# Mixer B of a hybrid encoder: a projection piece ahead of each odd step's transposes, q's transposes behind a piece, and the PSUM pools of the dense stages in the other order

## The chip, the cores and the metric

One core of one Trainium2 chip runs the whole program. The metric is the device time of one execution in microseconds (us); less is better. The engines are named PE (TensorE, matmuls; PEld is its weight load), DVE (VectorE), ACT (ScalarE), POOL (GpSimd) and SP (SyncE, which issues most DMAs here). PSUM is the memory that PE writes; it has eight banks of 128 x 512 fp32.

## The reference

Two layers over 1024 tokens of width 1024. Layer 0 uses mixer A (neighbourhood attention over a 16 x 64 grid), layer 1 mixer B (grouped-query attention). After each mixer stands a dense stage.

```python
for i in range(DEPTH):                                   # DEPTH = 2
    h = rms_norm(x, norm_g[i])
    y = mixer_a(h, ...) if i % 2 == 0 else mixer_b(h, ...)
    x = x + y                                            # y = (o * silu(gate)) @ w_out
    g = sigmoid(rms_norm(x, ple_norm_g[i]) @ ple_w_gate[i])
    x = x + g * (p[i] @ ple_w_proj[i])
return rms_norm(x, final_norm_g)

def mixer_b(h, ...):                                     # 16 query heads, 4 k/v heads, head size 64
    q, k, v, gate = split(h @ w_in)                      # 1024, 256, 256, 1024 columns
    q, k = rope(rms_norm(q)), rope(rms_norm(k))
    o = softmax(q @ k.T / 8) @ v                         # all 1024 tokens see all 1024
    return (o * silu(gate)) @ w_out
```

## The kernel before

Products are made in fp32r with each operand split in a high and a low half (names ending in h and l, or KA and KB): a product is high x high, high x low and low x high. ACT makes a high half by a copy, DVE the low half by a subtraction. The weights come by DMA into `wstage`, ACT splits off `wh` (L226) and DVE `wl` (L231).

The stages follow each other: mixer A, `dense_phase(0)`, mixer B, `dense_phase(1)`. Each opens its own PSUM pools, and pools take banks in the order in which they are opened. Mixer A opens `d` (2 banks), `s` (2), `t` (2) and then `o` (2); mixer B `d` (1 bank), `s` (2 tiles of 2 banks), `t` (2 tiles of 1 bank) and `o` (1); a dense stage `t` (4) and `d` (4). The first four blocks of a dense stage (`strassen_out`) are written to `d` tiles, the next four to `t` tiles.

**Mixer B** goes through 128 steps; a step is one query head, one half of the tokens and one block of 128 queries. Step n has these parts:

- scores, `f_S`: four matmuls of 128 x 512 into an `s` tile (KA, then KB), and DVE's minimum over it (`mn`, L1198). They are issued two steps ahead: step n issues those of n+2.
- exponentials, `f_E`: ACT, from `s` to `P` (L1204), issued one step ahead.
- transposes, `f_T`: eight transposes of `P` into two `t` tiles (L1214), each tile copied by ACT to PTh (L1216), and the rest by DVE to PTl (L1217).
- PV, `f_AV`: at every even n, for the steps n-2 and n-1 together, eight matmuls with PTh and eight with PTl into the `o` tile of the head (`o<-PTh,V` and `o<-PTl,V`). A new `o` tile is opened for every head and half, so at every second PV. When the head is done, ACT copies a part of it (L519) and DVE joins it (`Y<-o,Y`, L483), some items later.
- `q_stack`, at every eighth step: four transposes of q into one `t` tile (L1168), ACT's copy of it (L1170), and some items later the scaled halves QS by ACT (L1177) and DVE (L1178).

An even step issues: PV, exponentials of n+1, transposes of n, scores of n+2. An odd step issues: transposes of n, exponentials of n+1, scores of n+2, and at n = 3, 11, 19, ... a q_stack.

Between these, `mix(att, dense)` places **pieces** of other PE work: the projections of the next q, k and v (twelve matmuls of 128 x 256, half of a token tile), of the gates and of p (six matmuls of 128 x 512, L606 is ACT's copy of the last kind). All are written to the one `d` tile; the last piece of a tile is followed by ACT's copies (L1080 and L1044 for q, L1136 for k and v). Items of `att` and pieces have weights (`CB` for even steps with PV, `CN` for others; 1300 to 1316 for a piece), and after each item as many pieces follow as keep the two sums in proportion. The four calls of `mix` take 32 steps each, with 24, 50, 32 and 32 pieces. In the last one the last `HOLD` = 2 pieces are kept for behind the last step. Each item is followed by `pulse()`, which counts down the timers of `post`, the queue of deferred small operations. `leave` defers the copies of a finished piece behind an exponential that comes next.

After the steps `strassen_out` of the dense stage begins with `block(Y[0], ...)`; before mixer B, `dense_phase(0)` ends with transposes of the normalised rows by `to_ht` (L467, ACT's copy L468, DVE's subtraction L469); the last of these transposes are issued between mixer B's first pieces (`kv_items`).

Of the kernel before, what the change touches and what calls it, by code (L numbers as in the profile page):

```python
# [18 lines left out]
PSUM = bass.MemoryType.PSUM  # L19
# [20 lines left out]
HOLD = 2  # L40
# [118 lines left out]
def trunk(ctx, tc, x, wts, rpb, gains, hgains, mask, rope, gain0, out):  # L159
# [183 lines left out]
    def pulse():  # L343
        WQ.pump()
        post.tick()
# [13 lines left out]
            while self.left:  # L359
                self.left.pop(0)()  # L360

    leave = Evac()

    def mix(att, dense, lead=0, hold=0):
        for f, _ in dense[:lead]:
            f()
            pulse()
        kept = dense[len(dense) - hold:]
        dense = list(dense[lead:len(dense) - hold])
        total = sum(c for _, c in dense)  # L370
        span = sum(c for _, c in att)
        spent = done = 0.0
        for i, (f, c) in enumerate(att):
            f()
            leave.run()
            pulse()
            done += c
            while dense and spent < total * done / span - 1e-6:
                leave.run()
                leave.wait = i + 1 < len(att) and getattr(att[i + 1][0], "first", False)  # L380
                d, c = dense.pop(0)
                d()
                leave.wait = False
                spent += c
        leave.run()
        for f, _ in dense + kept:
            f()
            pulse()
# [598 lines left out]
    def mixer_b(pend):  # L987
        with ExitStack() as es:
# [174 lines left out]
            def q_stack(pair, hf):  # L1163
                g = pair // 2
                ps = psT.tile([128, 4, 128], F32, name="t")
                c = slice((pair % 2) * 128, (pair % 2) * 128 + 128)
                for t in range(4):
                    pe.transpose(ps[:, t], QT[g, hf][:, t, c], ident)  # L1168
                raw = sb.tile([128, 512], F32, name="th")
                act.activation(raw, ps.rearrange("p t c -> p (t c)"), AF.Copy)  # L1170
                for j in range(2):
                    own, oth = slice(64 * j, 64 * j + 64), slice(64 - 64 * j, 128 - 64 * j)
                    qs = sb.tile([128, 512], F32R, name="QS", bufs=3)
                    QST[2 * pair + j, hf] = qs

                    def high(qs=qs, own=own, oth=oth):
                        act.activation(qs[own], raw[own], AF.Copy)  # L1177
                        post.add(DQ, lambda: dve.tensor_tensor(qs[oth], raw[own], qs[own], ALU.subtract))  # L1178
                    if pro[0]:
                        high()  # L1180
                    else:
                        post.add(QO[j], high)
# [3 lines left out]
            steps = [(2 * p + j, hf, t) for p in range(8) for hf in range(2) for j in range(2) for t in range(4)]  # L1186

            def f_S(h, hf, t):
                g = h // 4
                ps = psS.tile([128, 1024], F32, name="s")  # L1190
                qt = QST[h, hf][:, t * 128:(t + 1) * 128]
                for kk, kt in enumerate((KA[g], KB[g])):
                    for c in range(2):
                        mm(ps[:, c * 512:(c + 1) * 512], qt, kt[:, c * 512:(c + 1) * 512], kk == 0, kk == 1)
                if t == 0:
                    RS[h, hf] = sb.tile([128, 4], F32, name="rs", bufs=3)
                mn = sb.tile([128, 1], F32, name="mn", bufs=3)
                dve.tensor_reduce(mn, ps, axis=AX.X, op=ALU.min)  # L1198
                P[h, hf, t] = (ps, mn)

            def f_E(h, hf, t):
                ps, mn = P[h, hf, t]
                p = sb.tile([128, 1024], F32, name="P")
                act.activation(p, ps, AF.Exp, bias=mn, scale=-1.0, accum_out=RS[h, hf][:, t:t + 1])  # L1204
                P[h, hf, t] = p

            def f_T(h, hf, t):
                p = P.pop((h, hf, t))
                c = slice((t % 2) * 128, (t % 2) * 128 + 128)
                for b in range(2):  # L1210
                    ps = psT.tile([128, 4, 128], F32, name="t")
                    for i in range(4):
                        k = 4 * b + i
                        pe.transpose(ps[:, i], p[:, k * 128:(k + 1) * 128], ident)  # L1214
                    ks = slice(4 * b, 4 * b + 4)
                    act.activation(PTh[:, ks, c], ps, AF.Copy)  # L1216
                    dve.tensor_tensor(PTl[:, ks, c], ps, PTh[:, ks, c], ALU.subtract)  # L1217
# [4 lines left out]
            def f_AV(h, hf, t):  # L1222
                if t == 1:
                    OP[h, hf] = psO.tile([128, 512], F32, name="o")
                o = OP[h, hf][:, (t - 1) * 128:(t + 1) * 128]
                for k in range(NT):
                    mm(o, V[h // 4][:, k], PTh[:, k], t == 1 and k == 0, False)
                for k in range(NT):
                    mm(o, V[h // 4][:, k], PTl[:, k], False, t == 3 and k == NT - 1)
                if t == 3:  # L1230
                    fin = head_end(sb, h, hf, RS[h, hf], OP.pop((h, hf)), ylive, 1, gg, talloc)
                    if fin:
                        later.add(FIN[1], fin)
# [18 lines left out]
            def exps(n):  # L1252
                def f():
                    f_E(*steps[n])
                f.first = True
                return f
            for g in range(4):
                att = []
                for n in range(32 * g, 32 * g + 32):
                    h, hf, t = steps[n]  # L1260
                    av = n >= 2 and n % 2 == 0
                    w = CB if av else CN
                    def turn():
                        if WQ.gate:
                            WQ.gate = False
                        later.tick()
                    att.append((turn, w[0]))
                    if av:
                        att.append((lambda n=n: f_AV(*steps[n - 1]), w[1]))
                    te = [(lambda n=n: f_T(*steps[n]), w[2])]  # L1270
                    if n + 1 < len(steps):
                        te.append((exps(n + 1), w[3]))
                    if n % 2 == 0 and n > 0:
                        te.reverse()
                    att += te
                    if n + 2 < len(steps):
                        def scores(n=n):
                            f_S(*steps[n + 2])
                            WQ.gate = n % 2 == 1 if n < 112 else None
                        att.append((scores, w[4]))  # L1280
                    m = n + QS_AT
                    if m % 8 == 0 and m < len(steps):
                        hn, fn, _ = steps[m]
                        att.append((lambda hn=hn, fn=fn: q_stack(hn // 2, fn), 0.0))
                    if YLOAD_B <= n < YLOAD_B + NT:
                        att.append((lambda t=n - YLOAD_B: load_y(1, t), 0.0))
                if g == 3:
                    att.append((lambda: f_AV(*steps[-1]), CB[1]))
                def gates(p):
                    return [i for hf in range(2) for i in gate_items("bg", p, hf, dalloc, sb, gg)]  # L1290
                dense = []
                if g > 0:
                    dense += left
                if g < 3:
                    qi = q_items(g + 1, pool)
                    kv = kv_items(1, pool) if g == 1 else [None, None]
                    dense += kv[:-2] + qi[:KS] + [k for k in kv[-2:-1] if k] + qi[KS:8] + [k for k in kv[-1:] if k] + gates(2 * g + 1) + qi[8:]
                    left = gates(2 * g + 2)
                else:
                    WQ.cap[3] = 2  # L1300
                    dense += gates(2 * g + 1) + pp_items(1, dalloc, sb, TAGS_B)
                mix(att, dense, hold=HOLD if g == 3 else 0)
            post.flush()
            later.flush()
            post.flush()
# [182 lines left out]
    def dense_phase(l):  # L1488
        with ExitStack() as es:
            one = es.enter_context(tc.tile_pool(name="done", bufs=1))  # L1490
            ps_t = es.enter_context(tc.tile_pool(name="dpt", bufs=4, space=PSUM))
            ps_d = es.enter_context(tc.tile_pool(name="dps", bufs=4, space=PSUM))
            wp2 = es.enter_context(tc.tile_pool(name=f"wp2{l}", bufs=2))
            X = [one.tile([128, D], F32, name=f"X{t}") for t in range(NT)]
            WQ.alloc[2] = lambda: [wp2.tile([128, 1024], F32R, name=f"w{c}2") for c in "hl"]
# [263 lines left out]
```

## Time and profile before

| | us |
|---|---|
| median of 3 timed runs | 1531.45 |
| lowest and highest of them | 1528.62, 1531.79 |
| the profiled execution, its own time | 1530.75 |
| its span, first to last instruction | 1528.9 |
| PE busy in it | 1499.4 (98%) |
| VectorE busy in it | 1102.1 (72%) |
| ScalarE busy in it | 899.4 (59%) |

In a row of the timeline stand the start and the duration in us, engine, line and operation, what is written and read, and how many instructions are merged into the row; in brackets the idle time of the engine just before, and what ended it. Matmuls overlap each other, so the duration of a row is longer than the time by which it puts off the next one. A row of waits gives total us, how often, and the longest. A row of stretches gives the bounds, the length, then busy time and instructions of PE, PEld, DVE, ACT and POOL, the granted clock of PE, the DMA engines' busy share and GB/s.

### The profile page before, as it was taken

How to read it: one execution, taken by the hardware profiler on the slowest of the kernel's cores; microseconds unless marked ns; L12 is line 12 of the kernel's file. 1: busy time of each engine (PE TensorE's matmuls, PEld its weight loads, DVE VectorE, ACT ScalarE, POOL GpSimd, SP SyncE). 2: the span in 40 equal slices, each digit the busy share in tenths (PEclk: the TensorE clock that was granted, in tenths of full speed). 3: DMA queues.
4: the chain of work that ended last, by engine and by line, in shares of the span. 5: the costliest groups of instructions: out<-in, count | busy, mean ns of one | idle time of the engine just before them, and what ended most of it. 6: DMA issues, size and time to landing. Idle time of an engine off the chain costs nothing.

```text
span 1528.9 us, 24361 instructions
## 1 busy us (share of the span) xinstructions
PE 1499.4 (98%) x8976; PEld 1314.0 (86%) x8976; DVE 1102.1 (72%) x2091; ACT 899.4 (59%) x1801; POOL 304.4 (20%) x413
## 2 busy tenths in 40 slices
PE   8999999999999999999999999999999999999997
PEld 8888988988988888888988889989899888878786
DVE  7566576477477599767887786777877877789856
ACT  6565465466366635433467676676767777745432
POOL 1222232142112000010222132453141300000022
PEclk9999999999999999999999999999999999999999
DMA  8325355272122962262210111111101122763123
GB/s 256 119 95 140 83 142 162 63 165 85 36 87 66 334 247 97 90 201 79 77 49 21 32 39 50 46 32 43 58 27 47 37 77 70 234 225 115 67 88 134
DMA packets 91096, 157.22 MB, mean 103 GB/s; under 512 B 18144, under 2 KB 54112, under 8 KB 90464
## 3 DMA queue, kind: packets, MB, share of 16 engines
q1 hardware_dynamic: 85824, 139.66, 27.9%
q0 software_dynamic: 2560, 8.39, 3.2%
q10 hardware_dynamic: 2592, 7.61, 1.4%
q8 instruction: 71, 1.16, 0.3%
q14 instruction: 49, 0.40, 0.1%
HBM read 125.10 MB, written 50.83 MB: 115 GB/s over the span
## 4 chain that ended last, share of the span: by engine, by line
PE 80%; DVE 11%; ACT 5%; issue 2%; DMA 1%; SPq 0%; ACTq 0%; DVEq 0%
PE d L317 50%; PE o L317 10%; PE s L317 8%; PE t L1214 6%; PE t L758 3%; DVE PTl L1217 2%; PE t L317 1%; PE t L467 1%; DVE mn L1198 1%; DVE xn L1541 1%; ACT PTh L1216 1%; ACT P L1204 1%; ACT wh L226 1%; DVE X L1437 1%; DVE HTl L1383 1%
## 5 line engine op out<-in xcount | busy, mean ns | idle before, releaser
L317 PE MATMUL d<-wh,HTh 128*128 128x256 f32 (+1 forms) x1032 | 343.3, 335 | 6.0 <-DVE HTl L469 2.3
L317 PE MATMUL d<-wh,HTl 128*128 128x256 f32 (+1 forms) x1032 | 338.3, 330 | 0.3 <-DVE HTl L469 0.3
L317 PE MATMUL d<-wl,HTh 128*128 128x256 f32 (+1 forms) x1032 | 337.0, 328 | 0.0
L1217 DVE TENSOR_TENSOR PTl<-t,PTh 128x512 fp32r<-128x512 f32 x256 | 164.4, 683 | 111.4 <-ACT PTh L1216 111.1
L317 PEld LDWEIGHTS d<-wh,HTh 128*128 128x128 f32 x1032 | 195.1, 190 | 25.8 <-DVE HTl L469 2.5
L317 PEld LDWEIGHTS d<-wl,HTh 128*128 128x128 f32 x1032 | 194.9, 190 | 19.0
L317 PEld LDWEIGHTS d<-wh,HTl 128*128 128x128 f32 x1032 | 195.1, 190 | 18.7 <-DVE HTl L469 0.5
L317 PE MATMUL d<-HTh,wh 128*128 128x512 f32 x504 | 206.0, 409 | 0.0
L317 PE MATMUL d<-HTh,wl 128*128 128x512 f32 x504 | 198.3, 394 | 0.0
L317 PE MATMUL d<-HTl,wh 128*128 128x512 f32 x504 | 197.6, 392 | 0.0
L1204 ACT ACTIVATE P<-s,mn 128x1024 f32<-128x1024 f32 x128 | 142.8, 1116 | 67.5 <-DVE mn L1198 66.7
L1216 ACT ACTIVATE PTh<-t 128x512 fp32r<-128x512 f32 x256 | 139.7, 593 | 45.1 <-PE t L1214 44.6
L1198 DVE TENSOR_REDUCE mn<-s 128x1 f32<-128x1024 f32 x128 | 154.7, 1209 | 12.3 <-PE s L317 12.3
L1214 PE MATMUL t<-ident,P 128*128 128x128 f32 x1024 | 137.2, 275 | 4.8 <-DVE PTl L1217 1.7
L317 PE MATMUL s<-KA,QS 128*128 128x512 f32 (+2 forms) x384 | 133.7, 402 | 0.0
L1214 PEld LDWEIGHTS t<-ident,P 128*128 128x128 f32 x1024 | 114.7, 140 | 20.1 <-DVE PTl L1217 12.6
L231 DVE TENSOR_TENSOR wl<-wstage,wh 128x1024 fp32r<-128x1024 f32 x78 | 101.7, 1308 | 34.7 <-ACT wh L226 34.2
L317 PE MATMUL s<-KB,QS 128*128 128x512 f32 (+2 forms) x384 | 121.8, 371 | 0.0
L317 PE MATMUL o<-PTh,V 128*128 128x256 f32 (+2 forms) x672 | 118.9, 288 | 1.2 <-DVE Y L483 0.9
L317 PE MATMUL o<-PTl,V 128*128 128x256 f32 (+2 forms) x672 | 119.1, 288 | 0.1
L762 DVE TENSOR_TENSOR PTl<-t,PTh 128x384 fp32r<-128x384 f32 (+1 forms) x128 | 66.6, 520 | 71.3 <-ACT PTh L761 70.1
L317 PEld LDWEIGHTS d<-HTh,wl 128*128 128x128 f32 x504 | 94.7, 188 | 21.6
(237 smaller groups left out, 2700.9 us busy)
## 6 DMA issues: line engine op xcount, KB each, us to landing
wstage<-in_wts SPq DMA_DIRECT2D x88, 512.0 KB
pp<-ppD SPq DMA_DIRECT2D x32, 256.0 KB
X<-in_x SPq DMA_DIRECT2D x15, 512.0 KB
rb<-rD SPq DMA_DIRECT2D x56, 128.0 KB
ppD<-th SPq DMA_DIRECT2D x20, 256.0 KB
tD0t<-in_wts SPq DMA_DIRECT2D x16, 256.0 KB
tD1t<-in_wts SPq DMA_DIRECT2D x16, 256.0 KB
xD<-X SPq DMA_DIRECT2D x8, 512.0 KB
```

Of the source, the lines that this page charges most:

```text
L226: act.activation(hi, s, AF.Copy)
L231: eng.tensor_tensor(lo[:, c:c + n], s[:, c:c + n], hi[:, c:c + n], ALU.subtract)
L317: pe.matmul(ps, a, b, start=first, stop=last, skip_group_check=True)
L467: pe.transpose(ps[:, k], xn[:, (4 * c + k) * 128:(4 * c + k + 1) * 128], ident)
L758: pe.transpose(ps[:, i], sp[:, i * 128:(i + 1) * 128], ident)
L762: dve.tensor_tensor(PTl[:, sl], ps[:, :m], PTh[:, sl], ALU.subtract)
L1198: dve.tensor_reduce(mn, ps, axis=AX.X, op=ALU.min)
L1204: act.activation(p, ps, AF.Exp, bias=mn, scale=-1.0, accum_out=RS[h, hf][:, t:t + 1])
L1214: pe.transpose(ps[:, i], p[:, k * 128:(k + 1) * 128], ident)
L1216: act.activation(PTh[:, ks, c], ps, AF.Copy)
L1217: dve.tensor_tensor(PTl[:, ks, c], ps, PTh[:, ks, c], ALU.subtract)
L1383: dve.tensor_tensor(al(t + m, c), src[m], ah(t + m, c), ALU.subtract)
```

## The change

`blocks(n)` names a step's transposes: "blocks" for even n, "apart" for odd n. `mix` notes in `since` whether a piece has come since the last transposes. Ahead of an "apart" item with none since, it issues the next piece; when no other piece is left, one of the kept ones, as long as more than two are there. That piece counts as spent. `HOLD` of the last call is raised by one. `after` is a second deferring queue that always waits: a q_stack goes into it and is issued behind the next piece, or at the end of the call. In `dense_phase`, the `d` pool is opened ahead of the `t` pool.

```diff
-    leave = Evac()
+    leave, after = Evac(), Evac()
+    after.wait = True
 
     def mix(att, dense, lead=0, hold=0):
         ...
+        since = True
         for i, (f, c) in enumerate(att):
+            kind = getattr(f, "kind", None)
+            if kind == "apart" and not since and (dense or len(kept) > 2):
+                d, e = (dense or kept).pop(0)
+                d()
+                spent += e
+                after.run()
+            if kind in ("apart", "blocks"):
+                since = False
             f()
             leave.run()
             pulse()
             done += c
             while dense and spent < total * done / span - 1e-6:
                 ...
                 d()
                 leave.wait = False
                 spent += c
+                since = True
+                after.run()
         leave.run()
+        after.run()
         for f, _ in dense + kept:
             f()
             pulse()
         ...
+            def blocks(n):
+                def f():
+                    f_T(*steps[n])
+                f.kind = "apart" if n % 2 else "blocks"
+                return f
         ...
-                    te = [(lambda n=n: f_T(*steps[n]), w[2])]
+                    te = [(blocks(n), w[2])]
         ...
-                        att.append((lambda hn=hn, fn=fn: q_stack(hn // 2, fn), 0.0))
+                        att.append((lambda hn=hn, fn=fn: after(lambda: q_stack(hn // 2, fn)), 0.0))
         ...
-                mix(att, dense, hold=HOLD if g == 3 else 0)
+                mix(att, dense, hold=HOLD + 1 if g == 3 else 0)
         ...
     def dense_phase(l):
+            ps_d = es.enter_context(tc.tile_pool(name="dps", bufs=4, space=PSUM))
             ps_t = es.enter_context(tc.tile_pool(name="dpt", bufs=4, space=PSUM))
-            ps_d = es.enter_context(tc.tile_pool(name="dps", bufs=4, space=PSUM))
```

## The prediction

> **What bounds the kernel now.** I read the page's busy shares first, then the busy time of the stretch that the change reorders (mixer B's 128 steps, 777 to 1344 us), then who waits for whom, then PE's timeline there and at the three hand-overs between stages.
>
> ```profile
> PE 1499.4 (98%) x8976; PEld 1314.0 (86%) x8976; DVE 1102.1 (72%) x2091; ACT 899.4 (59%) x1801; POOL 304.4 (20%) x413
> 777.00:1344.00 567.00, 557.83 (x3808) 501.51 (x3807) 423.58 (x663) 402.21 (x747) 137.90 (x212) 1.00 0.18 57
> PEld t L1214 <- DVE PTl L1217: 12.6, 36, 1.3
> ```
>
> TensorE bounds nearly everything: 98% busy, in mixer B 557.83 of 567 us, at full clock (1.00). VectorE has 423.58 us of work there and ScalarE 402.21, so neither is full, but each is the second link of a short loop. A step's eight transposes (L1214) fill the two PSUM tiles `t`; ScalarE copies each to PTh (L1216), VectorE subtracts to PTl (L1217), and only then is a `t` tile free. The third row is what that costs where it shows: the load of the next transposes waited 36 times, 12.6 us in all. There is no other large pot, so what can be won is waits of tenths of a microsecond, many times over.
>
> Busy time hides such waits, because matmuls overlap; I therefore count from start to start. A step that does not wait (T 20, scores, a piece, T 21, scores), and then one wait:
>
> ```profile
> 860.65 0.71 PE L317 MATMUL s<-KA,QS 128*128 128x512 f32 x2
> 861.66 0.28 PE L317 MATMUL d<-wh,HTh 128*128 128x256 f32 x1
> 863.09 1.04 PE L1214 MATMUL t<-ident,P 128*128 128x128 f32 x8
> 863.88 0.71 PE L317 MATMUL s<-KA,QS 128*128 128x512 f32 x2
> 865.59 1.19 PE L317 MATMUL o<-PTh,V 128*128 128x256 f32 x8 [0.54 <-DVE Y L483]
> ...
> 864.76 0.68 DVE L483 SCALAR_TENSOR_TENSOR Y<-o,Y 64x512 f32<-64x512 f32 x1
> ```
>
> Scores take 1.01 (861.66 - 860.65), a piece 1.43, transposes 0.79. The scores at 863.88 take 1.71, so PV waited 0.70: it opens a new `o` tile, of which there is one, and VectorE's join of the old head (L483) ended at 865.44.
>
> **The change part by part.** *Pieces ahead of an odd step's transposes.* Nothing is added or removed on any engine; pieces change places. I worked mix()'s two budgets through with the weights CB, CN and the pieces' costs. Group 0 has 24 pieces on 16 pairs of steps, so every second pair has none between its two transposes; group 1 has 50 and group 2 has 32, and there nearly every pair has one already; group 3 has 32 less those held. So "apart" puts a piece forward in only ten places: n = 1, 5, 9, 13, 17, 101, 113, 115, 125, 127. In the order of before, the transposes of n and n+1 have only the scores between them at n = 0, 4, 8, 12, 16, 102, 104 and 124, and nothing at all at 126; after it, at none of these. n = 8 is the usual one, 124 the worst of the eight:
>
> ```profile
> 810.75 1.04 PE L1214 MATMUL t<-ident,P 128*128 128x128 f32 x8
> 811.54 0.70 PE L317 MATMUL s<-KA,QS 128*128 128x512 f32 x2
> 812.75 1.26 PE L1214 MATMUL t<-ident,P 128*128 128x128 f32 x8
> ...
> 1328.35 0.71 PE L317 MATMUL s<-KA,QS 128*128 128x512 f32 x2
> 1330.19 1.25 PE L1214 MATMUL t<-ident,P 128*128 128x128 f32 x8 [0.67 <-DVE PTl L1217]
> 1332.44 0.67 DVE L483 SCALAR_TENSOR_TENSOR Y<-o,Y 64x512 f32<-64x512 f32 x1
> 1333.61 1.11 PE L317 MATMUL o<-PTh,V 128*128 128x256 f32 x8
> ```
>
> At n = 8 the scores take 1.21 instead of 1.01 (the first tile is late) and the transposes 1.26 instead of 1.04 (the second is): 0.42 lost. A piece of 1.43 covers both. Six places at 0.42 (4, 8, 12, 16, 102, 104): **2.5**. At n = 124 it is 0.83 + 0.21, but PV 125 then meets the join, which ends at 1333.11 against PV's start at 1333.61; that leaves **0.4**. The ends:
>
> ```profile
> 777.85 0.71 PE L317 MATMUL s<-KA,QS 128*128 128x512 f32 x2
> 780.19 0.98 PE L1214 MATMUL t<-ident,P 128*128 128x128 f32 x7 [1.16 <-ACT P L1204]
> 778.93 1.11 ACT L1204 ACTIVATE P<-s,mn 128x1024 f32<-128x1024 f32 x1
> 778.10 1.22 DVE L231 TENSOR_TENSOR wl<-wstage,wh 128x1024 fp32r<-128x1024 f32 x1 [0.26 <-PE t L1214]
> ...
> 1336.90 1.03 PE L1214 MATMUL t<-ident,P 128*128 128x128 f32 x8
> 1339.02 1.25 PE L1214 MATMUL t<-ident,P 128*128 128x128 f32 x8 [1.08 <-DVE PTl L1217]
> 1340.42 1.33 PE L317 MATMUL o<-PTh,V 128*128 128x256 f32 x8
> ```
>
> At n = 0 the wait is for the exponentials of step 1, to 780.04. The piece put ahead needs the low half of its weights, which VectorE has at 779.32, so it starts its second matmul about 0.5 late, and of the 1.33 between 778.86 (777.85 + 1.01, scores done) and 780.19 the net is **0.9** (0.9 to 1.3). At 126 the transposes take 2.12 instead of 0.79; a third held piece goes between: **1.3**. T 127 to PV 127 (1.40) stays: that is the copy's own latency. Together 5.1.
>
> The same order puts PV right behind its step's scores where a piece stood between: ten new places (1, 5, 9, 13, 17, 99, 111, 113, 115, 125). Such a place exists at n = 21 (0.70 lost, above) and at n = 25, where nothing is lost:
>
> ```profile
> 880.45 0.71 PE L317 MATMUL s<-KA,QS 128*128 128x512 f32 x2
> 881.47 0.76 PE L317 MATMUL o<-PTh,V 128*128 128x256 f32 x5
> ```
>
> So 0 to 7.0. The two differ in VectorE's queue: at 21 a query's low half (L1178, 0.69) stands ahead of the join. The change moves that too (next part), and at n = 9 to 17 and 111 to 115 it isn't there; I take **0.8**, for the weight splits in group 3.
>
> *q's transposes behind a piece.* All 15 q_stack calls now run behind the next piece, 2 to 6 turns of the post queue later. Their four transposes use one `t` tile, freed by ScalarE's copy:
>
> ```profile
> 789.40 0.71 PE L317 MATMUL s<-KA,QS 128*128 128x512 f32 x2
> 790.77 0.63 PE L1168 MATMUL t<-ident,qt 128*128 128x128 f32 x4 [0.20 <-DVE PTl L1217]
> 791.16 0.36 PE L317 MATMUL d<-wh,HTh 128*128 128x256 f32 x1
> 791.44 0.60 ACT L1170 ACTIVATE th<-t 128x512 f32<-128x512 f32 x1
> 792.87 0.38 ACT L1080 ACTIVATE qt<-d 128x256 f32<-128x256 f32 x1 [0.83 <-PE d L317]
> 793.28 0.42 ACT L1044 ACTIVATE t<-qt 128x256 f32<-128x256 f32 x1
>   DVE PTl L1217: 3.8, 8
> ```
>
> Removed: the wait ahead of q (1.37 instead of 1.01 here; 3.8 us in eight idles by PE and its weight load together, which partly overlap): **3.3**. Added: in seven places (48, 72, 80, 88, 96, 104, 112 by the head they serve) the piece behind which q now goes stands right ahead of a step's transposes. Those need both tiles, and the second is q's. The copy starts 0.67 after q and takes 0.60, so the tile is free 1.27 after q starts, and is wanted at 0.39 (q) + 0.40 = 0.79: 0.5 lost. Where that piece ends its tile (80, 96), its own evacuation (0.38 + 0.42) goes first on ScalarE, from about 0.2 behind the piece, and the loss is about 0.85; at 48 it is a k/v tile with a third copy, about 1.1. Four at 0.5, two at 0.85, one at 1.1: **4.8**. The deferred scaling to QS (L1177, L1178) still comes eight turns or more before the scores that read it; and coming later it leaves the join's place, so most of the present PV waits (0.70 at n = 21, and its like at 29 and 101) go: **1.2**, between 0 and 1.5. The rope-table loads on SP that a piece issues move with it by one item; POOL, 137.90 busy of 567, waits for them, and PE does not.
>
> *PSUM pools of the dense stages.* Pools take banks in the order they are opened. Before, `t` had banks 0-3 and `d` 4-7; after, the reverse. What matters is whose bank the next stage's first tile falls on.
>
> ```profile
> 708.20 0.60 PE L467 MATMUL t<-ident,xn 128*128 128x128 f32 x4
> 711.11 0.39 PE L317 MATMUL d<-wh,HTh 128*128 128x256 f32 x1 [2.31 <-DVE HTl L469]
> 710.37 0.69 DVE L469 TENSOR_TENSOR HTl<-t,HTh 128x512 fp32r<-128x512 f32 x1
> ...
> 530.14 0.60 ACT L606 ACTIVATE G<-d 128x512 f32<-128x512 f32 x1 [1.27 <-PE d L317]
> 530.72 0.69 DVE L536 TENSOR_TENSOR Y<-Y,t 128x512 f32<-128x512 f32 x1
> 531.51 0.47 PE L317 MATMUL d<-wh,HTh 128*128 128x512 f32 x1 [1.46 <-ACT G L606]
> ...
> 1346.32 0.40 PE L317 MATMUL d<-wh,HTh 128*128 128x512 f32 x1
> 1346.57 0.60 ACT L606 ACTIVATE th<-d 128x512 f32<-128x512 f32 x1 [1.79 <-PE d L317]
> ```
>
> Dense stage 0 to mixer B (708 us): B's first k/v piece is in bank 0, which the last `t` tile of the dense stage holds until VectorE's L469 ends at 711.06. Afterwards bank 0 was a `d` tile released three tiles ago, and the piece can start when the transposes are issued, about 708.65: **2.4** (2.0 if the whole `d` pool has to be free). The next pieces and the transposes shift with PE; ScalarE's and VectorE's work there hangs on PE's. Mixer A to dense stage 0 (531 us): the first block is on bank 4, mixer A's `t`, read by L536 until 531.41; afterwards on bank 0, free with L606 at 530.74: **0.7** (1.45 if it is the other of two `d` tiles). Mixer B to dense stage 1 (1346 us): now bank 4 is free and the block starts at once; afterwards bank 0 is the `d` tile that the last piece fills, free with L606 at 1347.17: **0.9 lost**. The Trainium skill (Perfetto Trace Analysis, section Matmuls) says that independent matmul groups should rotate through different PSUM banks, so that the evacuation of one runs beside the matmuls of the next. It speaks against the new order at the last of these places, where the trace bears it out; read for itself it would count both mixer ends as losses and put this part at 2.4 - 0.7 - 0.9 = 0.8 instead of 2.2.
>
> **Sum.** 5.1 - 0.8 + 1.2 + 3.3 - 4.8 + 2.2 = 6.2 us less. The profiled execution took 1530.75 (span 1528.9), so 1524.5; the three timed runs have a median of 1531.45 and span 1528.62 to 1531.79, so the profiled one stands 0.7 under the median, well inside them. I keep **1524.5**. About 0.2% (3.1 us) is what a measurement can tell from no change.
>
> **The rivals.**
> 1. *The next link takes over.* With TensorE ahead, each of the odd steps meets VectorE's join or ScalarE's copies instead: the 2.5 + 0.4 and the 1.2 are not had. For it: at n = 124 and 21 the join is what ends last. Against it: at n = 8 PV started well behind it. 1530.75 - 6.2 + 4.1 = 1528.7. Chance 0.15.
> 2. *The swap of pools frees nothing.* If B's first piece waits at 708 for something else that ends with L469, the 2.4 and the 0.7 go and the 0.9 is paid: 1530.75 - 6.2 + 3.1 = 1527.7. For it: one row names L469 and none names the bank. Against: the start stands 0.05 behind L469's end, and that instruction's output is not read by this piece. Chance 0.12.
> 3. *Slower: q's copy jams the odd transposes.* In the seven places q's tile is the second one of the transposes right behind it. If ScalarE has an exponential (1.11) and a piece's evacuation ahead of the copy, each costs 0.5 + 1.11 + 0.8 = 2.4, so 16.8 instead of 4.8: 1530.75 - 6.2 + 12.0 = 1536.6. Without q the rest gains 11.0, so it decides from 11.0 / 7 = 1.6 a place; over 0.2% slower from 2.0. Against it: the exponential of that step is issued behind the transposes, and the earlier one ahead of the even step's. Chance 0.10.
> 4. *Moved, not removed.* Each piece put forward is missing a step later, and the ten new PV places each pay the 0.70 of n = 21: 1530.75 - 6.2 + 6.2 = 1530.7, no change. Chance 0.10.
>
> **How the numbers follow.** The forecast has 0.53. Faster by over 0.2% (under 1527.7) holds nearly all of it (0.51), half of rival 2, a third of rival 1 and little of the others: 0.66. Slower holds most of rival 3 and the tails of 1 and 4: 0.11. No change: 0.23. The low end takes the good bounds together: 0.4 more at n = 0, 0.6 at 124, 0.3 at the joins, 0.75 at 531, 0.8 at the new PV places and 1.8 at q (all seven at 0.5, and the whole 3.8 removed): 4.7 lower, 1519.8, rounded down to 1519.5. The high end reaches over rivals 1 and 2 up to rival 4's edge: 1530. Rival 3 and half of rival 4 are left out.
>
> **What would show it.** The first k/v piece at about 0.45 behind the last transposes of dense stage 0 and no wait on L469 there; the first block of dense stage 1 about 0.9 behind the last piece, waiting for ScalarE's L606. In mixer B no L1214 start 1.2 behind scores at n = 4, 8, 12, 16; the pot of waits on L1217 down from 12.6 to about 6; L1168 no longer waiting for L1217, but in seven places transposes waiting for ScalarE's L1170, 0.5 to 1.1 each. Wrong would be: PV waiting for L483 in more places than now, L1170 waits over 1.6 each, or a wait of 2 us left at the start of mixer B.

## The result, and the profile after

| | before | after |
|---|---|---|
| median of six runs, us | 1531.37 (1528.62 to 1531.79) | 1524.69 (1523.32 to 1526.17) |
| ratio to before, 95% interval | | 0.9961 (0.9951 to 0.9971) |
| profiled execution, its span, us | 1530.75, 1528.9 | 1525.28, 1523.4 |

By the ratio the kernel became 6.0 us faster (4.4 to 7.5 by the interval; the two medians are 6.7 apart); the forecast was 6.2 less, or 1524.5. The profile page's row of busy times after, and two rows of who waits for whom:

```profile
PE 1496.9 (98%) x8976; PEld 1314.9 (86%) x8976; DVE 1096.4 (72%) x2091; ACT 899.8 (59%) x1801; POOL 303.8 (20%) x413
...
PEld t L1227 <- DVE PTl L1230: 6.7, 17, 1.3
PEld t L1227 <- ACT th L1183: 4.5, 7, 1.0
```

Lines have moved by 13: the transposes are L1227, PTl L1230, q's transposes L1181, their copy L1183. PE does the same work as before (x8976). The pot of waits on PTl is about halved (12.6 us in 36 waits before), and a new one has come: seven waits on the copy of q. Written T n for the first transposes of step n, mixer B wins 5.6 us from T 0 to T 35, loses 2.8 from there to T 98, and wins 1.0 from there to T 127.

The three hand-overs between stages in PE's timeline, each the start of the old stage's last matmul or transposes and of the new stage's first matmul. After:

```profile
529.49 0.39 PE L317 MATMUL d<-wh,wl 128*128 128x512 f32 x1
530.62 0.50 PE L317 MATMUL d<-wh,HTh 128*128 128x512 f32 x1 [0.74 <-ACT G L619]
...
707.32 0.60 PE L480 MATMUL t<-ident,xn 128*128 128x128 f32 x4
708.17 0.39 PE L317 MATMUL d<-wh,HTh 128*128 128x256 f32 x1 [0.25 <-ACT th L1617]
...
1339.63 0.39 PE L317 MATMUL d<-wh,KB 128*128 128x512 f32 x1
1340.75 0.50 PE L317 MATMUL d<-wh,HTh 128*128 128x512 f32 x1 [0.74 <-ACT th L619]
```

Of before, the two last matmuls whose followers the prediction shows:

```profile
529.67 0.39 PE L317 MATMUL d<-wh,wl 128*128 128x512 f32 x1
...
1346.09 0.39 PE L317 MATMUL d<-wh,KB 128*128 128x512 f32 x1
```

Mixer A to dense stage 0 takes 1.13 instead of 1.84, dense stage 0 to mixer B 0.85 instead of 2.91, mixer B to dense stage 1 1.12 instead of 0.23: 0.71 and 2.06 won, 0.89 lost.

Step 8 after, with a piece between scores and transposes, then PV behind the scores of step 11; and step 126:

```profile
806.01 1.03 PE L1227 MATMUL t<-ident,P 128*128 128x128 f32 x8
806.80 0.70 PE L317 MATMUL s<-KA,QS 128*128 128x512 f32 x2
809.23 1.04 PE L1227 MATMUL t<-ident,P 128*128 128x128 f32 x8
810.02 0.71 PE L317 MATMUL s<-KA,QS 128*128 128x512 f32 x2
811.03 1.11 PE L317 MATMUL o<-PTh,V 128*128 128x256 f32 x8
...
1330.26 1.03 PE L1227 MATMUL t<-ident,P 128*128 128x128 f32 x8
1332.65 1.03 PE L1227 MATMUL t<-ident,P 128*128 128x128 f32 x8
1334.04 1.23 PE L317 MATMUL o<-PTh,V 128*128 128x256 f32 x8 [0.35 <-ACT PTh L1229]
```

From 806.80 to 809.23 are 2.43: scores (1.01) and a piece (1.42), no wait; both sets of transposes take 0.79. PV follows 1.01 behind its scores, and the join (L496, from 809.79 for 0.68) ended at 810.47, ahead of it. At 126 transposes, piece and transposes take 3.78 to PV; less 1.40 for the piece that is 2.38 instead of 3.52, so 1.14 won.

Where q lands right ahead of transposes (T 44, behind a k/v piece):

```profile
961.07 0.60 PE L1181 MATMUL t<-ident,qt 128*128 128x128 f32 x4
961.33 0.38 ACT L1149 ACTIVATE th<-d 128x256 f32<-128x256 f32 x1 [1.13 <-PE d L317]
961.50 0.60 PE L1227 MATMUL t<-ident,P 128*128 128x128 f32 x4
...
962.25 0.57 ACT L1183 ACTIVATE th<-t 128x512 f32<-128x512 f32 x1
962.88 0.66 PE L1227 MATMUL t<-ident,P 128*128 128x128 f32 x4 [0.78 <-ACT th L1183]
963.29 0.71 PE L317 MATMUL s<-KA,QS 128*128 128x512 f32 x2
```

ScalarE evacuates the piece first (L1149, then L1057 at 961.74 and L1155 at 961.96), then q's tile (L1183); only then has the second half of the transposes a tile. From 961.50 to 963.29 are 1.79 instead of 0.79. Four such places lose 0.47 each (T 69, 85, 100 and 109), two 0.76 (T 77 and 93), this one 1.00: 4.4 in sum.

Two places of the last group of steps in which the forecast was too kind: PV behind T 113, and T 103.

```profile
1273.52 0.69 DVE L496 SCALAR_TENSOR_TENSOR Y<-o,Y 64x512 f32<-64x512 f32 x1
1274.23 1.23 DVE L231 TENSOR_TENSOR wl<-wstage,wh 128x1024 fp32r<-128x1024 f32 x1
1274.35 1.19 PE L317 MATMUL o<-PTh,V 128*128 128x256 f32 x8 [0.31 <-DVE Y L496]
1275.38 1.28 DVE L1230 TENSOR_TENSOR PTl<-t,PTh 128x512 fp32r<-128x512 f32 x2
1276.11 1.33 PE L317 MATMUL o<-PTl,V 128*128 128x256 f32 x8 [0.58 <-DVE PTl L1230]
...
1226.29 1.22 DVE L231 TENSOR_TENSOR wl<-wstage,wh 128x1024 fp32r<-128x1024 f32 x1
...
1228.86 1.28 DVE L1230 TENSOR_TENSOR PTl<-t,PTh 128x512 fp32r<-128x512 f32 x2
1229.60 0.93 PE L1227 MATMUL t<-ident,P 128*128 128x128 f32 x5 [0.91 <-DVE PTl L1230]
```

Both times a weight split (L231, 1.2 us) stands ahead of PTl in VectorE's queue, at T 103 with q's low half (L1191) and a head's last product (L574), 0.69 each, behind it. PE waits 0.58 and 0.91 for PTl; the 0.31 at 1274.35 is for the join (L496). Before, at n = 113:

```profile
1279.90 1.23 DVE L231 TENSOR_TENSOR wl<-wstage,wh 128x1024 fp32r<-128x1024 f32 x1
1280.89 1.11 PE L317 MATMUL o<-PTh,V 128*128 128x256 f32 x8
1281.04 1.28 DVE L1217 TENSOR_TENSOR PTl<-t,PTh 128x512 fp32r<-128x512 f32 x2
1281.84 1.28 PE L317 MATMUL o<-PTl,V 128*128 128x256 f32 x8
```

VectorE had the same order there, split ahead of PTl, but a piece stood between the scores and PV: PV's second half follows the first by 0.95, without a wait. It is PV's new place that lays the split bare.

**A caution on comparing profiles.** PE's order is the same in all kernels here up to mixer B's first transposes, yet the matmul that PE has at 66.15 us in the profile of before came between 64.42 and 66.43 in the ten others. This scatter goes with the granted clock: the seven profiles whose window from 10 to 20 us shows 0.83 come there at 65.85 to 66.43, the four with 1.00 at 64.42 to 65.03. So I measure from that matmul to the last one where two profiles are compared: 1454.34 before, 1449.06 after (5.3 less), and 1449.26 in the second profile of after (f4_after below).

### The profile page after: what moved, and what is told of

Same layout as the page of the kernel before. It is cut to its first block, busy times and chain, and to the rows that moved or that the text cites. A ratio compares the mean times of both kernels' runs of the same rounds, so it can differ in the third digit from the quotient of the medians.

```text
span 1523.4 us, 24376 instructions
## 1 busy us (share of the span) xinstructions
PE 1496.9 (98%) x8976; PEld 1314.9 (86%) x8976; DVE 1096.4 (72%) x2091; ACT 899.8 (59%) x1801; POOL 303.8 (20%) x413
## 4 chain that ended last, share of the span: by engine, by line
PE 43%; DVE 6%; ACT 2%; issue 1%; DMA 0%; POOL 0%; ACTq 0%; DVEq 0%; POOLq 0%
PE d L317 19%; PE o L317 9%; PE s L317 7%; PE t L1227 7%; PE t L317 1%; DVE xn L1560 1%; DVE PTl L1230 1%; DVE X L1456 0%; PE t L1181 0%; DVE wl L231 0%; DVE mn L1211 0%; DVE HTl L482 0%; DVE HTl L1402 0%; ACT PTh L1229 0%; ACT th L1183 0%
## 5 line engine op out<-in xcount | busy, mean ns | idle before, releaser
L1230 DVE TENSOR_TENSOR PTl<-t,PTh 128x512 fp32r<-128x512 f32 x256 | 165.1, 684 | 108.7 <-ACT PTh L1229 107.5
L1227 PE MATMUL t<-ident,P 128*128 128x128 f32 x1024 | 136.4, 274 | 5.2 <-ACT th L1183 2.9
L1227 PEld LDWEIGHTS t<-ident,P 128*128 128x128 f32 x1024 | 115.2, 140 | 16.6 <-DVE PTl L1230 6.7
L231 DVE TENSOR_TENSOR wl<-wstage,wh 128x1024 fp32r<-128x1024 f32 x78 | 100.3, 1290 | 34.9 <-ACT wh L226 34.4
```

The costliest lines, as they stand in the source:

```text
L231: eng.tensor_tensor(lo[:, c:c + n], s[:, c:c + n], hi[:, c:c + n], ALU.subtract)
```

## The experiments

Edits are given in short form; "..." stands for what is left out.

**The parts alone.** e1_pools is the kernel before with

```
-ps_t, ps_d      # order in which dense_phase opens its pools
+ps_d, ps_t
```

> The kernel before with the PSUM pools of the dense stages in the new order, and nothing else. Theory (the gain is a sum of separate small waits): only the three hand-overs move, by what the trace of after shows there: 0.71 won at mixer A to dense stage 0, 2.06 won at dense stage 0 to mixer B of which 0.3 is lost again before the first transposes, 0.89 lost at mixer B to dense stage 1: 1.6 to 1.9 us less than the kernel before, about 1529.6. Rival (the pools alone carry the result, the reordered steps cancel out): 5.5 to 6.5 us less, about 1525. Rival (hand-overs are given back by the next link): no change, 1531.4.

Measured: 1527.70 against 1529.78 of before on that chip, ratio 0.9986 (0.9978 to 0.9995), 2.1 less (0.8 to 3.4). In the trace the hand-overs are 1.12, 0.85 (705.87 to 706.72) and 1.13, as in after. From the 66 us matmul on it is 1.4 less. The pools are worth about a third of the result, not the whole and not nothing.

e2_pieces is the kernel before with the pieces only:

```
+ if kind == "apart" and not since and (dense or len(kept) > 2): ...   # a piece, then the odd transposes
+ mix(att, dense, hold=HOLD + 1 if g == 3 else 0)
```

> The kernel before with the pieces ahead of odd transposes (and one more held piece); q's transposes and the pools as before. Theory: at the nine places without a piece before, the trace of after shows 1.4 (n = 0), four times 0.44, 0.4 (n = 104), 0.3 (n = 124) and 1.1 (n = 126) won, 5.0 in all, and about 2.4 lost where the weighted value product now follows its scores at once in group 3 (n = 99, 101, 113, 125): 2.6 us less, and 0 to 1 us worse than that because q's low halves still stand ahead of the join at n = 5 and 13: 1529.2, between 1528.5 and 1530. Rival (moved, not removed): 1531.4, no change.

Measured: 1527.83, ratio 0.9991 (0.9982 to 1.0000), 1.4 less (0 to 2.8) where 2.6 was expected; by the times alone no change is not ruled out. Its profile has mixer B's 128 steps 3.6 shorter (T 0 to T 127), 0.7 of it at n = 67, more likely by chance (f3_best, below); so most was not merely moved. In this profile 1.3 of the gain was lost again ahead of the mixer, to the clock (last section). From T 4 to T 6 and from T 12 to T 14 it gains only 0.04 and 0.03 (0.4 in after): q's low halves stand ahead of the join there and PV waits for it, as expected.

e3_queue is the kernel before with the queue only:

```
- att.append((lambda ...: q_stack(hn // 2, fn), 0.0))
+ att.append((lambda ...: after(lambda: q_stack(hn // 2, fn)), 0.0))
```

> The kernel before with q's transposes behind the next piece; pieces and pools as before. Theory: 3.3 won ahead of q, 1.2 won at the joins, 4.0 to 4.4 paid by the transposes that now stand right behind q, up to 0.8 paid where q meets the keys' transposes at n = 52: no change, 1531.4, between 1530.4 and 1532.4. Rival (q's copy jams the odd transposes): each of the six to eight places costs 1.6 or more, 1537 or more. Rival (q's copy is hidden, its tile is free in time): 4.5 us less, 1527.

Measured: 1528.55, ratio 0.9994 (0.9985 to 1.0003): 0.9 less, -0.5 to 2.3: not to be told from the no change that was expected, and no jam. From the 66 us matmul on it is 2.0 less. The two sides show in the trace: up to T 35 it wins 3.9 on before and at n = 99 another 1.1; from T 35 to T 98 it gives 2.9 back. The rows of waits:

```profile
PEld t L1227 <- DVE PTl L1230: 11.3, 27, 1.3
...
PEld t L1227 <- ACT th L1183: 4.0, 6, 1.0
```

Mixer B's steps are 3.6 shorter with the pieces alone, 2.1 with the queue alone and 3.7 with both: they do not add up. In the last group (T 98 to T 127) either alone wins 1.0 to 1.3 and both together 1.0.

**What q's places cost.** e4_q_fix is the kernel after, but q waits only where no piece came since the last transposes:

```
+ if kind == "q":
+     after.wait = not since
```

> The kernel after, but q's transposes are put off only if no piece has been issued since the last transposes; otherwise they are issued at once. Theory: the right-behind-q places at n = 44, 68, 76, 84, 92 and 108 (1.00 + 0.47 + 0.76 + 0.47 + 0.76 + 0.47 in the trace of after, 3.9 in all) go, and the loss of about 0.6 near n = 52 with them; one at n = 100 stays; q waits for no tile, because a piece stands between. 3.5 to 4.5 us less than after, about 1520.7. Rival (q at once brings the low halves back into the join's place, or the wait ahead of q): 0 to 1.5 us less than after, 1523.2 to 1524.7.

Measured: 1520.44, ratio to before 0.9940 (0.9927 to 0.9952), where after has 0.9961; from the 66 us matmul on 4.4 less than after (4.6 than its second profile), 3.9 of it within mixer B's steps. Of the waits on q's copy, one is left (T 100), out of seven:

```profile
PEld t L1229 <- DVE PTl L1232: 5.8, 17, 1.3
...
PEld t L1229 <- ACT th L1185: 0.5, 1, 0.5
```

So the rival, that the early q brings other waits back, falls here.

**Whose bank.** f1_banks is the kernel after with

```
+ if l == 0: ps_d = four()          # four pools of one tile, used in turn
  ps_t = ...
+ if l == 1: ps_d = four()          # dense stage 1: old order
```

> The kernel after with two changes of the dense stages' PSUM: dense stage 1 opens its pools in the old order, and the `d` pool of four tiles is four pools of one tile, used in turn. Theory (a stage's first tile waits for whatever holds its bank, and a pool is given back as a whole): mixer B's first piece starts 0.45 instead of 0.85 behind the last transposes of dense stage 0, and dense stage 1's first block 0.23 instead of 1.12 behind the last piece: 1.3 us less than after. Rival (the 0.85 is the bank's own last reader, not the pool): the first start stays at 0.85, 0.9 less. Rival (the order of pools does not matter at mixer B's end): 1.12 stays.

Measured: 1524.13 against 1525.17 of after on the same chip (f4_after), ratios to before 0.9957 (0.9944 to 0.9969) and 0.9963 (0.9949 to 0.9977): the times can't tell them apart, the trace can.

```profile
706.29 0.60 PE L480 MATMUL t<-ident,xn 128*128 128x128 f32 x4
706.65 0.36 PE L317 MATMUL d<-wh,HTh 128*128 128x256 f32 x1
711.55 2.48 DVE L1739 SCALAR_TENSOR_TENSOR wstage<-X,stn,gain 128x1024 f32<-128x1024 f32 x2
714.19 0.38 ACT L1149 ACTIVATE th<-d 128x256 f32<-128x256 f32 x1 [4.83 <-PE t L480]
714.62 0.39 PE L317 MATMUL d<-wh,HTh 128*128 128x256 f32 x1 [1.10 <-ACT th L1149]
...
1338.56 0.39 PE L317 MATMUL d<-wh,KB 128*128 128x512 f32 x1
1338.79 0.40 PE L317 MATMUL d<-wh,HTh 128*128 128x512 f32 x1
```

Both theories of the place hold: B's first piece starts 0.36 behind the transposes instead of 0.85, so the wait was for the pool as a whole; and dense stage 1's block starts 0.23 behind the last piece, so the 0.89 was the order of pools. But the first of these is given back at once. The third piece starts 8.33 behind the transposes here (714.62 - 706.29) and 8.33 in after: it needs the first piece's tile, which ScalarE empties at 714.19. That row names PE's transposes, but they had ended by 713.52; ScalarE starts 0.16 behind the end of VectorE's last normalisation (L1739, to 714.03), here as in after (715.06, then 715.22), and the normalisation has not moved, 7.74 behind the same transposes in both. That it is what ScalarE waits for is read from this, not tested. The net gain from 66 us on is 1.2 to 1.4, 0.9 of it at mixer B's end.

**What took the time in the last group.** f2_splits is the kernel after with

```
- WQ.gate = n % 2 == 1 if n < 112 else None
+ WQ.gate = n % 2 == 1 if n < 126 else None
```

> The kernel after with the weight splits still allowed only behind an odd step's scores up to step 126, not step 112: VectorE's low half of a weight (1.23 us) goes behind PTl at n = 113 and n = 125 instead of ahead of it. Theory (what the weighted value products lost in group 3 is that split in VectorE's queue): the two halves of the product at n = 113 take 2.4 instead of 3.0 to 3.3, those at n = 125 lose 0.3 to 0.7 less; 1.0 us less than after in the trace (0.6 to 1.5), and nothing is late where the split goes, since a piece stands ahead of the next odd transposes. Rival (the join L496 itself is late, whatever stands behind it): no change. Rival (the split is missed one step later): no change in sum, with transposes at n = 115 or 127 late by as much.

Measured: 1524.38, ratio to before 0.9957 (0.9944 to 0.9969); in the trace mixer B's steps are 1.1 shorter, 0.95 of it at n = 113, 0.2 at n = 121, nothing at n = 125. The same place as above:

```profile
1274.48 1.29 DVE L1230 TENSOR_TENSOR PTl<-t,PTh 128x512 fp32r<-128x512 f32 x2
1274.59 1.19 PE L317 MATMUL o<-PTh,V 128*128 128x256 f32 x8 [0.31 <-DVE Y L496]
1275.62 1.12 PE L317 MATMUL o<-PTl,V 128*128 128x256 f32 x8
1276.91 1.21 DVE L231 TENSOR_TENSOR wl<-wstage,wh 128x1024 fp32r<-128x1024 f32 x1
```

The split stands behind PTl now, and the second half of PV follows the first by 1.03 instead of 1.76. The wait of 0.31 for the join stays. So the split was the larger part of the loss at n = 113, the join the smaller; at 125, where PV waits 0.53 for the join in after, the theory was wrong.

e7_group3 is the kernel after with "apart" left out of the last group but for n = 127:

```
- f.kind = "apart" if n % 2 else "blocks"
+ f.kind = "apart" if n % 2 and (n < 96 or n == 127) else "blocks"
```

> The kernel after without pieces put forward in the last group of steps, except at n = 127: at n = 101, 113, 115 and 125 the piece stands behind the odd step's scores again. Read in the trace, from the transposes of step 98 to those of step 127. Theory (in group 3 the pieces put forward were paid for by weighted value products that met the join, the weight split and PTl): the product at n = 113 gains 1.0 to 1.4 and those at n = 101 and 125 0.2 to 0.7 each, while the transposes of n = 101, 113, 115 and 125 lose 0.4 each and n = 125 up to 1.0: within 0.7 of after in sum, either sign. Rival (as the prediction had it, 0.8 lost against 0.4 a place won): the stretch is 1 to 2 us longer than in after.

Measured, in one execution alone: 1526.42 beside 1532.49 of before on that chip; from T 98 to T 127 it takes 0.56 longer than after, as the theory had it. At n = 115 and 125 the piece put forward is worth 0.2 and 0.3; from T 100 to T 104 and from T 112 to T 114 both orders take the same, to 0.02. There the gain is only moved. The 1.35 by which T 112 to T 114 grew against before comes back as 1.36, for another reason: PV has a piece ahead of it again and waits for no join, but T 113 has only scores ahead of it and waits 0.88 for PTl. So this run doesn't tell what the loss in after is; f2_splits and the rows of before do.

**All three together.** f3_best is the kernel after with the edits of e4, f1 and f2.

> All three together on the kernel after: q put off only if no piece came since the transposes, the dense pools as in the run on banks, the splits behind odd scores up to step 126. Theory (separate small waits add up): 4.4 (the q run against after, both read from 66 us on) + 1.3 + 1.0 = 6.7 us less than after, about 1518. Rival (waits take each other's place): less than 5 of the 6.7.

Measured: 1519.05 against 1525.17 (f4_after) and 1531.85 (before) on that chip, ratio to before 0.9922 (0.9909 to 0.9934). In the trace it is 5.6 to 5.8 less than after, not 6.7. Mixer B's steps are 0.4 shorter than in e4, where f2's edit alone brought 1.1, for the wait ahead of q at n = 67 is back (0.64). Here, then in e4_q_fix:

```profile
1074.21 1.30 POOL L579 TENSOR_TENSOR Y<-Y,rb 128x512 f32<-128x512 f32 x1 [5.70 <-DMA rb<-rD]
1074.33 1.72 DVE L595 SCALAR_TENSOR_TENSOR G<-th,G 128x512 f32<-128x512 f32 x1 [0.79 <-ACT th L591]
1076.81 0.63 PE L1183 MATMUL t<-ident,qt 128*128 128x128 f32 x4 [0.64 <-DVE PTl L1232]
...
1074.58 0.69 DVE L595 SCALAR_TENSOR_TENSOR G<-th,G 128x512 f32<-128x512 f32 x1 [0.80 <-ACT th L591]
1074.83 1.60 POOL L579 TENSOR_TENSOR Y<-Y,rb 128x512 f32<-128x512 f32 x1 [6.08 <-DMA rb<-rD]
```

VectorE's product L595 stands ahead of the PTl that q waits for. In f3_best GpSimd's product L579 has begun first, and L595 takes 1.72; in e4 L595 has begun first, takes 0.69, and L579 takes 1.60. All eleven profiles sort so: 1.57 to 1.75 in the five where GpSimd began first, 0.69 in the other six. L579 waits for a DMA (rb), so a few tenths in its landing decide. With q at this place the wait came in before (0.48), e1_pools (0.67) and f3_best, and not in e2_pieces or e4. The two profiles of after, one kernel, fall on different sides, so this is more likely chance than the edits; it is 0.8 of the 1 that the sum misses here. f3_best is the fastest version of this study.

> The kernel after, unchanged, on the same chip as the runs beside it, to compare them with: 1524.7 by its own runs, 0.9961 of the kernel before.

Measured: 1525.17, ratio 0.9963, as above.

## Why the prediction was right, point by point

- **Sum**: forecast 6.2 less, measured 6.0 (4.4 to 7.5), and 5.3 between the profiles from 66 us on. The mechanism, many waits of tenths, held. Terms were mis-sized and partly offset each other: the pieces came out about 0.5 worse, PV 0.7 worse and the pools 0.3 worse, q's waits and the joins 0.5 better. That the total came so near is in part luck.
- **Pieces ahead of odd steps** (5.1): n = 0 gave 1.36 (0.9): its piece did not wait for the low half of its weights. Places 4, 8, 12, 16 gave 0.43, 0.42, 0.45, 0.46 (0.42 each), 124 and 125 together 0.3 (0.4), 126 1.14 (1.3). At 102 and 104 together nothing came (0.84): PTl of n = 102 is late behind a split, q's low half and a head's last product.
- **PV right behind its scores** (0.8 lost): no wait at n = 1, 5, 9, 13, 17, 111 and 115, 0.2 at 99. At n = 113, 1.35 is lost between T 112 and T 114, of which f2 puts 0.95 on the weight split. The cause was the one foreseen, PV behind its scores where a split of group 3 stands ahead of PTl, but mis-sized: 0.8 was taken for all ten places, and one alone cost more.
- **Joins** (1.2): n = 21 and 29 lost their waits (0.70 and 0.31), n = 101 a third of a microsecond. e2 shows the other side: without the queue n = 5 and 13 would have got such waits.
- **q's waits** (3.3 removed): e3's 3.9 up to step 35, joins included, and 1.1 at n = 99 are 5.0 for the 4.5 of both. **q's places** (4.8 paid): 4.4 in the trace, seven places with the three sizes foreseen (0.47, 0.76 and 1.00 for 0.5, 0.85 and 1.1). Not foreseen: 0.5 near n = 52, where q and the keys' transposes meet. e4, without six of the seven and without that meeting, wins 3.9.
- **Pools** (2.2): 0.71 + 2.06 - 0.89 = 1.9 (0.7 + 2.4 - 0.9). The first piece waited for the whole `d` pool, the alternative that I had given as 2.0. The Trainium skill (Perfetto Trace Analysis, section Matmuls), as the prediction reads its advice to rotate matmul groups through banks, would have had the new order lose at both mixer ends; that holds at mixer B's end (0.89 lost) and not at mixer A's, where the trace shows 0.71 won.
- **Rivals**: 2 and 3 fall with e1 and e3. Rival 4 is right at two places (T 100 to 104, T 112 to 114) and wrong elsewhere. Rival 1 holds at n = 113 and 125, where PV waits for the join (0.31 and 0.53), but PV waits for it in no more places than before (two, 0.9 in all); it is also what happened to f1's edit at 708 us.

## What to carry to other kernels

Where one engine is full and the rest is tenths of a microsecond, count from start to start at every place of the order, and price each moved step by what is queued ahead of the copy that frees its tile. A moved step pays at the place where it lands: put off only those that gain by it (e4: 4 us for two lines). Before opening pools, ask who reads the bank of the next stage's first tile last, and what the second link behind that wait is. Where two profiles differ by tenths at one place, look first whether an instruction there took longer, and what ran beside it.

## What the runs showed of the hardware

The granted clock fell once behind a short idle. In e2_pieces PE idled 2.3 us at 707 us, as in before and e3_queue, but only in this profile the matmuls behind it ran at half clock for 3 us: 0.213 from start to start for a 128x256 matmul instead of 0.12, 1.3 us lost. Windows of before, then of e2_pieces (after the five engines' busy times: granted clock, DMA share, GB/s):

```profile
711.00:714.10 3.10, 2.99 (x25) 2.99 (x26) 2.47 (x13) 0.27 (x2) 0.00 (x0) 1.00 0.42 169
```

```profile
709.30:712.40 3.10, 2.97 (x14) 2.97 (x15) 2.47 (x13) 0.29 (x2) 0.00 (x0) 0.50 0.42 169
```

The clock also differs near the start (0.83 or 1.00 from 10 to 20 us), and the two profiles of after, one of each kind, are 1.5 us apart by the matmul at 66 us. If the idle at 708 us is the occasion for the loss, the swap of pools, which shortens it, removes it as well; one profile doesn't show that, and how often it happens was not measured.

The Trainium skill (TensorE: Matmul & The Clock Gate, Part 1) says that the array's clock is either full or half and falls to half after about 3.4 us of idleness, judged in a free-running window. The half agrees with the 0.50 here, and that three profiles with the same idle differ fits a window that runs free; the idle of 2.3 us was shorter than the page's figure.

GpSimd and VectorE can hold each other up: of two products of 128x512 that overlapped (f3_best above), the one that began second took 1.72 us instead of 0.69 on VectorE, or 1.60 instead of 1.30 on GpSimd. Why, no run here shows.
